# The order of TensorE's work in the attention of a gated hybrid block: equal blocks of queries, other work in fixed shares

## The chip, the cores and the metric

The kernel runs on one core of one Trainium2 chip. The metric is the device time of one execution in microseconds; lower is better. Engines are named as the profile names them: PE is TensorE (PEld its weight loads), DVE is VectorE, ACT is ScalarE, POOL is GpSimd, and SP issues the DMAs.

## The reference

One layer over 1024 positions of width 1024, float32. After an RMS norm one wide projection gives all inputs of two branches: an mLSTM in both directions (4 heads of 256), and a differential attention (8 heads). Both branches are gated, projected, mixed by two sigmoid gates, and projected once more onto the residual. The change lies in the attention:

```python
def diff_attention(q, k, v, lam):
    ...
    def one_block(qb):
        scores = jnp.einsum('bqhjd,bkhjd->bhjqk', qb, k) * scale
        p = jax.nn.softmax(scores, axis=-1)
        p_diff = p[:, :, 0] - lam * p[:, :, 1]
        return jnp.einsum('bhqk,bkhd->bqhd', p_diff, v)
...
dq = apply_rope(b_q.reshape(B, S, DA_HEADS, 2, DA_QK_DIM), positions)
dk = apply_rope(b_k.reshape(B, S, DA_HEADS, 2, DA_QK_DIM), positions)
...
att = diff_attention(dq, dk, da_v, lam)
att = rmsnorm(att, da_subln_g[layer]) * (1.0 - lambda_init)
y_b = att.reshape(B, S, DA_WIDTH).astype(x.dtype) * jax.nn.silu(b_z)
```

Each head has two score maps (j = 0, 1) of 64 dimensions each, two softmaxes, one difference of them, and one product with v.

## The kernel before, in words

Every float32 product is made as three products of a high and a low part (`H`, `L`). The kernel runs in stages: the norm and the first projections; the mLSTM's inputs; the attention of 8 heads; the mLSTM; the rest of the gates; the two branch products, the mix and the output product.

**Units.** `build` (L1429) puts PE's work together as a list of `Unit`s (L46): a cost in us of PE, a function that issues the instructions, and names by which a planner knows them. `MM` = 0.214 is the cost of one matmul of 512 columns, `TP` = 0.109 that of a transpose. `run` (L386) goes through the finished list in order; it loads a weight block one key ahead of its first use (`load_w`, L177: a DMA, a cast on ACT, a subtraction on POOL). In the attention only PE's order is written by hand; the order on ACT, DVE and POOL is chosen by the framework when the program is built.

**The attention's units of head h** (`da_parts`, L906), for a block t of 128 queries:

- S(t), L923: twelve matmuls for both score maps into two PSUM tiles of two banks each (tag `S`); then on DVE two maxima over 1024 keys (L926), on ACT two exponentials (L928), on DVE the difference (L932 to L934). Cost 6 MM.
- T(t, g), g = 0 and 1, called T0 and T1: four transposes (L131) of the difference into one bank of tag `T`; ACT copies the high part (`pH`, L947), DVE takes the low part (`pL`, L948).
- PV(pair, g), called PV0 and PV1: twelve matmuls each (L959) of two blocks of queries with v; both write one bank of tag `T`, which ACT copies to `att` (L961) at the end.
- M(pair): two transposes of `att` into a bank of tag `T`, and two squares on ACT in place (L971), with sums; behind the fourth M of a head POOL makes the norm and multiplies the gate `zg` by `att` (L975 to L981).
- G(half): four transposes that spread the norm into a bank of tag `T`; DVE multiplies it into `zg` (L991), and SP stores `zg`.

There are two banks of tag `T` for T, PV, M and G together, and two of tag `pj` for all projections.

**The block's order** (`da_cycle`, L1006): S(t) of this head first; M at even t; G of the head before at t = 4 and 5; PV0 and PV1 at odd t; then T0 and T1 of the block before. M(2), M(3) and the last PV of a head fall into the next head's blocks 0 to 2.

**The other work** of a head is a list of its own, in this order: the rope projections of q and k of the next head (`da_proj`, L842: 32 units of 3 MM, in two halves of 512 positions; behind each half come products on DVE, L852 to L864, sums and differences on POOL, L865 to L869, casts on ACT, L868, and DMAs); for odd heads the projection of v for two heads (`da_v`, 32 units of 6 TP); for even heads the z projections (L880, L881) of the head before, ahead of the rope, and of this head, behind it; z of head 0 is made before the attention; head 0 takes one gate projection, head 7 three (`gate_units`, L831).

**The planner** (`Weaver`, L62) holds a model of the time. `weave` merges the main list of a head (the units of the eight blocks, one behind the other) with the other list: at each step it puts the unit that is ready first, and among those ready the one that is less far on in its own list by cost. `ready` (L68) knows of named predecessors with a lag each (`after`, `LAG`) and of banks: a unit with a tag isn't ready before one of the tag's banks is free, by the model's `hold` of its last users (2.2 us for T and G, 3.7 for PV, 8.1 for M). `put` adds a unit to the list and moves the model's time on.

Of the kernel before, what the change touches and what calls it, by code (L numbers as in the profile page):

```python
# [13 lines left out]

S = 1024
D = 1024
# [3 lines left out]
L = 256  # L20
NC = S // L
NB = L // 128
# [6 lines left out]
def two_pi_parts():  # L29
# [9 lines left out]
MM = 0.214  # L39
TP = 0.109  # L40

LAG = dict(Th=2.2, Sh=5.0, PVh=3.7, Mh=8.1, qk=14.0, T=6.8, PV=3.7, M=4.5, F=6.0, TTh=1.9, TT=3.2, POh=1.6,
           PO=1.7, Wh=0.3, W=2.0, STh=2.1, ST=4.9, th=1.8, t=4.1, aq=9.0, outh=6.6, out=14.0, G=6.0)
# [18 lines left out]
class Weaver:  # L62
# [28 lines left out]
    def weave(self, *lists):  # L91


        lanes = {}
        for i, un in enumerate(lists):
            total, c = sum(u.cost for u in un) or 1.0, 0.0
            for u in un:
                lanes.setdefault((i, u.lane), []).append((c / total, u))
                c += u.cost
        self.coming = {u.name for un in lists for u in un if u.name}  # L100
        heads = list(lanes.values())
        while heads:
            best = min(heads, key=lambda l: (max(self.ready(l[0][1]), self.now), l[0][0]))
            u = best.pop(0)[1]
            self.put(u)
            self.coming.discard(u.name)
            heads = [l for l in heads if l]


class Block:  # L110
# [199 lines left out]
    def big(self, n, dt=F32):  # L310
        return self.s0.tile([128, S + 4], dt, name=n, tag="big", bufs=6)

# [30 lines left out]
    def conv_sink(self, seg, n):  # L343
# [3 lines left out]
        def sink(i, j, ps, rest):  # L347
            if i not in box:
                box[i] = (self.big("cin"), [])
                p.memset(box[i][0][:, 0:2], 0.0)  # L350
                p.memset(box[i][0][:, S + 2:S + 4], 0.0)
            raw, got = box[i]
# [9 lines left out]
            w = lambda j: self.conv[:, j * 16 + base:j * 16 + base + 1]  # L362
            y = self.big("y")[:, 0:S]
            for half in range(2):
# [247 lines left out]
    def angles(self, an):  # L612
# [38 lines left out]
        for src in (cs, sn):  # L651
            reps.append(self.big("rep")[:, 0:S].rearrange("p (k a b) -> p k a b", k=8, a=4))
            for k in (0, 4):
# [252 lines left out]
    def da_parts(self, h, st):  # L906
        v, a, p, q, w1 = self.v, self.a, self.p, self.q, self.w1

        def scores(t):
            if t == 0:  # L910
                st["Z"] = w1.tile([128, 2, 8], F32, name="Z", tag="Z", bufs=2)
                st["ms"] = w1.tile([128, 8], F32, name="ms", tag="ms", bufs=2)
                st["att"] = w1.tile([128, S], F32, name="att", tag="att", bufs=1)
            qq, k = st["q", t // 4], st["k"]
            c = slice((t % 4) * 128, (t % 4) * 128 + 128)
            Z = st["Z"]
            both = [self.bank("S", (128, S)) for _ in range(2)]

            for o in (slice(0, 512), slice(512, S)):
                for m, (x, y) in enumerate(((0, 0), (0, 1), (1, 0))):  # L920
                    for j, ps in enumerate(both):
                        r = slice(64 * j, 64 * j + 64)
                        self.t.matmul(ps[:, o], lhsT=qq[r, x, c], rhs=k[r, y, o], start=(m == 0), stop=(m == 2))  # L923
            for j, ps in enumerate(both):
                nm = w1.tile([128, 1], F32, name="nm", tag="nm", bufs=3)
                v.tensor_reduce(out=nm, in_=ps, axis=AX.X, op=ALU.max, negate=True)  # L926
                e = w1.tile([128, S], F32, name=f"e{j}", tag=f"e{j}", bufs=2 if j == 0 else 1)
                a.activation(out=e, in_=ps, func=AF.Exp, bias=nm[:, 0:1], accum_out=Z[:, j, t:t + 1])  # L928
                st["e", j] = e
            e0 = st["e", 0]  # L930
            r = w1.tile([128, 1], F32, name="r", tag="r", bufs=1)
            v.reciprocal(out=r, in_=Z[:, 1, t:t + 1])  # L932
            v.tensor_scalar(out=r, in0=r, scalar1=Z[:, 0, t:t + 1], scalar2=self.nlam[:, 0:1], op0=ALU.mult, op1=ALU.mult)
            v.scalar_tensor_tensor(out=e0, in0=e, scalar=r[:, 0:1], in1=e0, op0=ALU.mult, op1=ALU.add)  # L934
            st["p", t] = e0

        def transposes(t, g):
            pt = st["p", t]
            s = slice((t % 2) * 128, (t % 2) * 128 + 128)
            if t % 2 == 0:  # L940
                st["pT", t // 2, g] = (w1.tile([128, 4, 256], F32R, name="pH", tag="pH", bufs=2),
                                       w1.tile([128, 4, 256], F32R, name="pL", tag="pL", bufs=2))
            pH, pL = st["pT", t // 2, g]
            ps = self.bank("T", (128, 4, 128))
            for i in range(4):
                self.tr(ps[:, i, :], pt[:, (4 * g + i) * 128:(4 * g + i + 1) * 128])
            a.copy(pH[:, :, s], ps)  # L947
            v.tensor_tensor(out=pL[:, :, s], in0=ps, in1=pH[:, :, s].bitcast(F32), op=ALU.subtract)  # L948
# [14 lines left out]
        def squares(t2):  # L963
            pt = self.bank("T")
            for i in range(2):
                t = 2 * t2 + i
                self.tr(pt[:, i * 128:(i + 1) * 128], st["att"][:, t * 128:(t + 1) * 128])
            for i in range(2):
                t = 2 * t2 + i
                x = pt[:, i * 128:(i + 1) * 128]  # L970
                a.activation(out=x, in_=x, func=AF.Square, accum_out=st["ms"][:, t:t + 1])  # L971
            if t2 == 3:
                zz = w1.tile([128, 8], F32, name="zz", tag="zz", bufs=1)
                Z0 = st["Z"][:, 0, :]
                p.tensor_scalar(out=zz, in0=Z0, scalar1=EPS, scalar2=None, op0=ALU.mult)  # L975
                p.tensor_tensor(out=zz, in0=zz, in1=Z0, op=ALU.mult)
                rs = self.rsqrt(w1, st["ms"], 1.0 / 128.0, zz, "rb", eng=p)
                p.tensor_scalar(out=rs, in0=rs, scalar1=(1.0 - LAMBDA_INIT) * 0.5, scalar2=None, op0=ALU.mult)
                for half in range(2):
                    g = st["g", half]  # L980
                    p.tensor_tensor(out=g, in0=st["att"][:, half * 512:(half + 1) * 512], in1=g, op=ALU.mult)  # L981
                st["rs"] = rs

        def scale(half):
# [3 lines left out]
            for i in range(4):  # L988
# [3 lines left out]
            q.dma_start(out=self.yb[h][:, half * 512:(half + 1) * 512], in_=g)  # L992

        return dict(
            S=lambda t: Unit(6 * MM, lambda: scores(t), tag="S", hold=LAG["Sh"], name=("S", h, t), after=((("qk", h), LAG["qk"]),)),
            T=lambda t, g: Unit(4 * TP, lambda: transposes(t, g), tag="T", hold=LAG["Th"], name=("T", h, t, g),
                                after=((("S", h, t), LAG["T"]),)),
            PV=lambda t2, g: Unit(12 * TP, lambda: pv(t2, g), tag="T" if g == 0 else None, hold=LAG["PVh"], name=("PV", h, t2, g),
                                  after=((("T", h, 2 * t2 + 1, g), LAG["PV"]),)),
            M=lambda t2: Unit(2 * TP, lambda: squares(t2), tag="T", hold=LAG["Mh"], name=("M", h, t2),  # L1000
                              after=((("PV", h, t2, 1), LAG["M"]), (("z", h if t2 == 3 else -1), 0.0))),
            G=lambda half: Unit(4 * TP, lambda: scale(half), tag="T", hold=LAG["Th"], name=("G", h, half),
                                after=((("M", h, 3), LAG["F"]),)))
# [425 lines left out]
    def build(self):  # L1429
# [21 lines left out]
        with pool(name="const", bufs=1) as self.const, \  # L1451
# [51 lines left out]
            w = Weaver()  # L1503
            w.add(enter("h", "hpool"), enter("tab", "tab", side="right"), enter("tf", "tf", side="right"),
                  enter("p0", "p0", side="right"), banks("ps0", T=6), keep(E.PE, E.Activation, E.DVE, E.Pool), do(begin))
            k = self.PIECES
# [30 lines left out]
            for i, x in enumerate(products + [None]):  # L1537
                y = products[i - 1] if i else None
                un = sum(([x[0]] if x else []) + ([y[6]] if y else []) + ([x[3]] if x else []) + ([y[5]] if y else [])
                         + ([x[1], x[4], x[2]] if x else []), [])  # L1540
# [5 lines left out]
            qk, z = zip(*[self.da_proj(h, sts[h]) for h in range(NH_B)])  # L1546
            w.add(do(lambda: setattr(self, "ahead", True)), *qk[0], *z[0], *self.da_v(0, sts[0:2]))
            prev = None
            for h in range(NH_B):
                cur = self.da_parts(h, sts[h])  # L1550
                main = sum((self.da_cycle(cur, prev, t) for t in range(8)), [])
                ahead = qk[h + 1] if h + 1 < NH_B else []
                if h + 1 == NH_B:
                    nxt = fill(FILL[h]) + z[h]
                elif h % 2 == 1:
                    nxt = ahead + self.da_v((h + 1) // 2, sts[h + 1:h + 3]) + fill(FILL[h])
                else:
                    nxt = z[h - 1] + ahead + fill(FILL[h]) + z[h] if h else ahead + fill(FILL[0])
                w.weave(main, nxt)
                prev = cur  # L1560
            end = sum((self.da_cycle(None, prev, t) for t in range(6)), [])
            w.weave(end[:-2], fill(2))
# [25 lines left out]
            k = len(passA) // 2  # L1588
# [52 lines left out]
```

## Time and profile before

| | us |
|---|---|
| median of 3 runs | 1708.58 |
| the runs | 1706.8 to 1708.61 |
| the profiled execution, its own time | 1706.56 |
| its span, from the first to the last instruction | 1704.7 |
| the attention's eight heads in it | about 455 to 1075 |

The mean clock granted to PE is 0.994. In a row of the timeline the first number is the start in us from the span's beginning, the second the duration; then the engine, the line of the kernel, the operation, the tile written and the tiles read, the count, and in brackets the idle time of the engine just before and what ended it. Matmuls overlap in their pipeline, so the distance from start to start tells their price, not the duration. In the tile names S are scores, T is any bank of tag `T` (T<-ident,att is M, T<-ident,rb_y is G, T<-ident,e is T0 or T1), and pj is a projection.

### The profile page before, as it was taken

How to read it: one execution, taken by the hardware profiler on the slowest of the kernel's cores; microseconds unless marked ns; L12 is line 12 of the kernel's file. 1: busy time of each engine (PE TensorE's matmuls, PEld its weight loads, DVE VectorE, ACT ScalarE, POOL GpSimd, SP SyncE). 2: the span in 40 equal slices, each digit the busy share in tenths (PEclk: the TensorE clock that was granted, in tenths of full speed). 3: DMA queues.
4: the chain of work that ended last, by engine and by line, in shares of the span. 5: the costliest groups of instructions: out<-in, count | busy, mean ns of one | idle time of the engine just before them, and what ended most of it. 6: DMA issues, size and time to landing. Idle time of an engine off the chain costs nothing. (4 is left out here: it accounts for less than half of the span.)

```text
span 1704.7 us, 25425 instructions
## 1 busy us (share of the span) xinstructions
PE 1654.3 (97%) x9431; PEld 1389.8 (82%) x9431; DVE 988.3 (58%) x1799; ACT 777.0 (46%) x1554; POOL 606.5 (36%) x680
## 2 busy tenths in 40 slices
PE   7999999999999999999999999999999899999998
PEld 5777887887877987898788878899999777888887
DVE  5778668674377666666666655226666633135533
ACT  7454555553265455454545455325655644022221
POOL 5767676665243134413241331221330312212000
PEclk9999999999999999999999999999999999999999
DMA  5334444334231213221231222175464327344222
GB/s 181 98 121 130 137 123 132 116 124 146 65 81 44 63 38 87 56 69 38 75 81 32 62 62 75 50 208 155 143 170 137 109 89 237 117 147 136 87 91 83
DMA packets 175630, 178.79 MB, mean 105 GB/s; under 512 B 12185, under 2 KB 135410, under 8 KB 175506
## 3 DMA queue, kind: packets, MB, share of 16 engines
q1 hardware_dynamic: 174594, 175.58, 34.5%
q8 instruction: 74, 1.21, 0.3%
q10 hardware_dynamic: 912, 1.59, 0.2%
q14 instruction: 50, 0.41, 0.1%
HBM read 114.11 MB, written 46.24 MB: 94 GB/s over the span
## 5 line engine op out<-in xcount | busy, mean ns | idle before, releaser
L429 PE MATMUL pj<-hH,wH 128*128 128x512 f32 x640 | 266.8, 417 | 3.3 <-ACT f L542 1.5
L429 PE MATMUL pj<-hH,wL 128*128 128x512 f32 x640 | 252.0, 394 | 1.8 <-POOL wL L207 1.8
L429 PE MATMUL pj<-hL,wH 128*128 128x512 f32 x640 | 250.8, 392 | 0.2 <-DVE hL L580 0.2
L209 POOL TENSOR_TENSOR wL<-raw,wH 128x1024 fp32r<-128x1024 f32 x41 | 99.7, 2431 | 291.9 <-ACT wH L204 289.5
L928 ACT ACTIVATE e<-S,nm 128x1024 f32<-128x1024 f32 x128 | 142.5, 1115 | 96.1 <-DVE nm L926 96.0
L926 DVE TENSOR_REDUCE nm<-S 128x1 f32<-128x1024 f32 x128 | 150.5, 1218 | 8.5 <-PE S L923 7.8
L429 PEld LDWEIGHTS pj<-hH,wH 128*128 128x128 f32 x640 | 121.0, 189 | 37.9 <-issue 14.5
L451 PE MATMUL pj<-wH,hH 128*128 128x256 f32 x512 | 149.9, 293 | 0.3
L948 DVE TENSOR_TENSOR pL<-T,pH 128x512 fp32r<-128x512 f32 x128 | 87.9, 689 | 105.8 <-ACT pH L947 104.9
L451 PE MATMUL pj<-wL,hH 128*128 128x256 f32 x512 | 144.8, 283 | 1.4 <-POOL wL L207 1.4
L429 PEld LDWEIGHTS pj<-hH,wL 128*128 128x128 f32 x640 | 120.6, 188 | 30.3 <-POOL wL L207 3.2
L451 PE MATMUL pj<-wH,hL 128*128 128x256 f32 x512 | 144.5, 282 | 0.0
L429 PEld LDWEIGHTS pj<-hL,wH 128*128 128x128 f32 x640 | 121.3, 190 | 18.3 <-DVE hL L580 0.6
L429 PE MATMUL pj<-sl_yb,wH 128*128 128x512 f32 x384 | 121.8, 397 | 4.4 <-ACT sl_yb L1314 2.2
L947 ACT CAST pH<-T 128x512 fp32r<-128x512 f32 x128 | 74.8, 585 | 84.6 <-PE T L131 84.0
L204 ACT CAST wH<-raw 128x1024 fp32r<-128x1024 f32 x56 | 58.9, 1052 | 114.3 <-PE pj L429 88.1
L923 PE MATMUL S<-kst,qq 64*128 64x512 f32 x768 | 106.7, 408 | 0.0
L451 PEld LDWEIGHTS pj<-wH,hH 128*128 128x128 f32 x512 | 97.7, 191 | 5.5 <-issue 2.2
L451 PEld LDWEIGHTS pj<-wL,hH 128*128 128x128 f32 x512 | 97.5, 190 | 2.3 <-POOL wL L207 2.3
L451 PEld LDWEIGHTS pj<-wH,hL 128*128 128x128 f32 x512 | 97.7, 191 | 0.1
L429 PEld LDWEIGHTS pj<-sl_yb,wH 128*128 128x128 f32 x384 | 73.3, 191 | 22.5 <-DVE sl_yb L1315 3.3
L923 PEld LDWEIGHTS S<-kst,qq 64*128 64x128 f32 x768 | 67.8, 184 | 26.3 <-issue 10.5
(358 smaller groups left out, 4112.2 us busy)
## 6 DMA issues: line engine op xcount, KB each, us to landing
raw<-in_w_in_dram SPq DMA_DIRECT2D x88, 512.0 KB, 3.9
kst<-hl SPq DMA_DIRECT2D x64, 128.0 KB, 2.4
qq<-hl SPq DMA_DIRECT2D x64, 128.0 KB, 2.4
x<-in_x_dram SPq DMA_DIRECT2D x8, 512.0 KB, 6.1
cak<-y SPq DMA_DIRECT2D x16, 256.0 KB, 2.3
cakH<-cin SPq DMA_DIRECT2D x16, 256.0 KB, 4.4
cakL<-tz SPq DMA_DIRECT2D x16, 256.0 KB, 4.1
gm<-oz SPq DMA_DIRECT2D x16, 256.0 KB, 2.7
```

Of the source, the lines that this page charges most:

```text
L204: self.a.copy(wH, raw)
L209: self.p.tensor_tensor(out=wL, in0=raw, in1=wHf, op=ALU.subtract)
L429: self.t.matmul(ps, lhsT=l[:, k, :], rhs=r, start=(n == 0), stop=(n == 23))
L451: self.t.matmul(ps[:, i, :], lhsT=l, rhs=r[:, k, :], start=(kh == 0 and k == 0 and m == 0), stop=(kh == 1 and k == 3 and m == 2))
L923: self.t.matmul(ps[:, o], lhsT=qq[r, x, c], rhs=k[r, y, o], start=(m == 0), stop=(m == 2))
L926: v.tensor_reduce(out=nm, in_=ps, axis=AX.X, op=ALU.max, negate=True)
L928: a.activation(out=e, in_=ps, func=AF.Exp, bias=nm[:, 0:1], accum_out=Z[:, j, t:t + 1])
L947: a.copy(pH[:, :, s], ps)
L948: v.tensor_tensor(out=pL[:, :, s], in0=ps, in1=pH[:, :, s].bitcast(F32), op=ALU.subtract)
```

## The change

`weave` isn't used for the eight heads any more. A new method, `blocks`, takes the main units as eight blocks, and the other list. It gives each block the same length: the cost of all units of the head divided by eight. What a block's own units leave of that length is its room, and the room is dealt out behind its units in fixed shares: 2.0 behind S, 3.0 behind M, 0.5 behind G, none behind PV0, 1.5 behind PV1, 2.5 behind T0, 3.5 behind T1. Units of the other list are put, in their order, as long as half the next one's cost fits into what the shares have opened so far. `ready` isn't asked; what is left is added at the end. The cost of S in the planner goes from 6 MM to 8 MM. The units themselves, the order within a block, the other lists and all code after the attention stay.

```diff
+    SHARE = {"S": 2.0, "M": 3.0, "G": 0.5, "PV0": 0.0, "PV1": 1.5, "T0": 2.5, "T1": 3.5}
+
+    def blocks(self, blocks, other):
+
+        other = list(other)
+        length = (sum(u.cost for un in blocks for u in un) + sum(u.cost for u in other)) / len(blocks)
+        done = 0.0
+        for n, un in enumerate(blocks):
+            share = [self.SHARE.get(u.name[0] + (str(u.name[3]) if len(u.name) > 3 else ""), 0.0) if u.name else 0.0 for u in un]
+            main = sum(u.cost for u in un)
+            room, given = (n + 1) * length - done - main, 0.0
+            for k, u in enumerate(un):
+                self.put(u)
+                upto = room * sum(share[:k + 1]) / sum(share)
+                while other and given + other[0].cost / 2 <= upto:
+                    given += other[0].cost
+                    self.put(other.pop(0))
+            done += main + given
+        self.add(*other)
...
-            S=lambda t: Unit(6 * MM, lambda: scores(t), tag="S", hold=LAG["Sh"], name=("S", h, t), after=((("qk", h), LAG["qk"]),)),
+            S=lambda t: Unit(8 * MM, lambda: scores(t), tag="S", hold=LAG["Sh"], name=("S", h, t), after=((("qk", h), LAG["qk"]),)),
...
-                main = sum((self.da_cycle(cur, prev, t) for t in range(8)), [])
+                main = [self.da_cycle(cur, prev, t) for t in range(8)]
...
-                w.weave(main, nxt)
+                w.blocks(main, nxt)
```

## The prediction

> **What bounds the kernel now.** I read the page first, then the busy time of the attention's stretch, then who PE waits for, then the timelines around each wait.
>
> ```profile
> span 1704.7 us, 25425 instructions
> PE 1654.3 (97%) x9431; PEld 1389.8 (82%) x9431; DVE 988.3 (58%) x1799; ACT 777.0 (46%) x1554; POOL 606.5 (36%) x680
> ```
> ```profile
> 455.00:1075.00 620.00, 614.08 (x3898) 508.81 (x3897) 402.53 (x553) 313.70 (x650) 198.52 (x188) 1.00 0.23 62
> ```
> ```profile
> PE T L131 <- ACT T L971: 5.6, 6, 1.4
> PE T L131 <- DVE pL L948: 0.3, 1, 0.3
> ```
>
> The second fence is the stretch of all eight heads: length, then busy time of PE, weight load, DVE, ACT, POOL; the granted clock is 1.00. PE is the bound. It is idle for 620.00 - 614.08 = 5.9 us, and the two waits make up just that (5.6 + 0.3): six times a transpose (T) waits for a PSUM bank that the squares (L971, on ACT) of an M unit still hold. Nothing else in the attention is there to be won, since the change neither adds nor removes a matmul.
>
> One of the six, head 1, block t = 2:
>
> ```profile
> 538.35 1.66 PE L923 MATMUL S<-kst,qq 64*128 64x512 f32 x12
> 538.44 0.69 DVE L948 TENSOR_TENSOR pL<-T,pH 128x512 fp32r<-128x512 f32 x1 [0.45 <-ACT pH L947]
> 539.04 0.68 DVE L863 TENSOR_TENSOR hl<-pj,sinT 128x512 f32<-128x512 f32 x1
> 539.94 0.50 PE L429 MATMUL pj<-hH,wH 128*128 128x512 f32 x1
> 542.10 0.38 PE L131 MATMUL T<-ident,att 128*128 128x128 f32 x2
> 542.90 1.11 ACT L928 ACTIVATE e<-S,nm 128x1024 f32<-128x1024 f32 x1
> ```
> ```profile
> 545.26 0.39 PE L429 MATMUL pj<-hH,wL 128*128 128x512 f32 x1
> 546.29 0.65 PE L131 MATMUL T<-ident,e 128*128 128x128 f32 x4 [0.64 <-ACT T L971]
> ```
> ```profile
> 546.04 0.20 ACT L971 ACTIVATION_READ_ACCUMULATOR T<-T 128x1 f32 x1
> ```
>
> I count from the end of the scores S, here 539.94, where the first filler matmul starts. M (T<-ident,att) stands at 2.16, its squares end at 546.24 = 6.30, since ACT takes them behind both exponentials, and these (from 2.96) behind the rope copies of the next head's projection. T1 could have started at 545.26 + 0.23 = 545.49 = 5.55, so it loses 0.80, 0.16 more than the idle column shows, because the last matmul's modelled end runs on. With that, the six cost 5.6 + 6 x 0.16 = 6.6, the last 0.3 about 0.4: **7.0 us is all that can go.**
>
> **The change, part by part.** S's cost goes from 6 to 8 MM (1.712), which only feeds the planner's sums. The diff touches no line of z, so "all z in the attention" moves nothing by itself. What changes is the order: the old weave asked ready() before each unit and so kept T away from held banks; blocks() asks nothing and deals the other units by fixed shares. The other list keeps its own order, so the weights' keys, their loads, copies and subtractions stay in sequence, and SP's queue sees the same loads; yb's stores still wait for their own L991. The matmuls themselves cost what they did: 64 score groups, each between fillers of full height.
>
> The orders, by arithmetic. Head 2: main 8 x 1.712 + 16 x 0.436 + 8 x 1.308 + 4 x 0.218 + 2 x 0.436 = 32.9, other 64 x 0.642 = 41.1, so a block has 74.0 / 8 = 9.25. Block 4 has room 5.80 and shares S 2, M 3, G 0.5, T0 2.5, T1 3.5 of 11.5, which open 1.01, 2.52, 2.77, 4.03, 5.80. A unit goes out while given + 0.32 is within that: two after S, two after M (2.57 given), none after G (2.57 + 0.32 > 2.77), two, three. So: S 2 M 2 **G T0** 2 T1 3. Heads 1 to 7 all come out so at t = 4. Blocks 0 and 2: S 2 M 3 T0 2 T1 3; block 6: S 2 M 2 T0 3 T1 3; odd blocks: S 1 (G) PV0 PV1 1 T0 2 T1 2.
>
> *G then T0 at t = 4 (new).* There are two T banks. M holds one, G the other, and T0 comes directly. Rows of block 4 now, head 2 and then head 7 (no rope there):
>
> ```profile
> 639.51 0.50 PE L429 MATMUL pj<-hH,wH 128*128 128x512 f32 x1
> 640.98 0.38 PE L131 MATMUL T<-ident,att 128*128 128x128 f32 x2
> 641.12 0.48 PE L429 MATMUL pj<-hH,wH 128*128 128x512 f32 x1
> 641.89 0.60 PE L131 MATMUL T<-ident,rb_y 128*128 128x128 f32 x4
> 642.25 0.49 PE L429 MATMUL pj<-hH,wH 128*128 128x512 f32 x1
> 642.48 1.11 ACT L928 ACTIVATE e<-S,nm 128x1024 f32<-128x1024 f32 x1
> 642.60 0.75 DVE L991 SCALAR_TENSOR_TENSOR zg<-zg,cols,T 128x512 f32<-128x512 f32 x1 [0.45 <-PE T L131]
> 643.58 0.27 ACT L971 ACTIVATE T<-T 128x128 f32<-128x128 f32 x1
> 643.87 1.10 ACT L928 ACTIVATE e<-S,nm 128x1024 f32<-128x1024 f32 x1
> ```
> ```profile
> 645.15 0.19 ACT L971 ACTIVATION_READ_ACCUMULATOR T<-T 128x1 f32 x1
> ```
> ```profile
> 1039.84 0.50 PE L429 MATMUL pj<-hH,wH 128*128 128x512 f32 x1
> 1041.19 1.11 ACT L928 ACTIVATE e<-S,nm 128x1024 f32<-128x1024 f32 x1 [1.36 <-DVE nm L926]
> 1042.22 0.60 PE L131 MATMUL T<-ident,rb_y 128*128 128x128 f32 x4
> 1042.93 0.75 DVE L991 SCALAR_TENSOR_TENSOR zg<-zg,cols,T 128x512 f32<-128x512 f32 x1 [0.64 <-PE T L131]
> ```
> ```profile
> 1043.87 0.19 ACT L971 ACTIVATION_READ_ACCUMULATOR T<-T 128x1 f32 x1
> ```
>
> Two filler units behind S take 640.98 - 639.51 = 1.47; a third 0.69 (2.16 above). M (0.14) and one unit behind it (0.77) take 0.91, to 641.89; M and two 1.60. So G starts at 3.07. Its four transposes hand over after 0.36 (642.25), M's two after 0.14 (641.12), which is 0.11 each, 0.44 for four where a transpose follows: T0 could start at 3.51. G's bank is free when L991 ends, 643.35 - 641.89 = 1.46 after G's start (head 7: 1.46): 4.53. M's is free at 645.34 - 639.51 = 5.83 with rope and 1044.06 - 1039.84 = 4.22 without. T0 loses 0.7 (M's bank, head 7) to 2.3 (M's, with rope), by G's bank 1.02. I take 1.0, since the rows now show T0 on G's bank: seven heads, **+7.0**. Behind T0 stand on PE's queue T1, the fillers and the next scores, and ACT's copy of T0 waits for it; nothing hides it. A gain is excluded, for both banks are held.
>
> *T1 behind M, t = 2 of heads 1, 3, 5.* M now stands at 1.47, where the first square goes between the exponentials (fence above), and squares end 645.34 - 642.48 = 2.86 after the first exponential starts. T1 stands at 1.47 + 0.91 + 1.38 + 0.36 + 0.77 + 0.69 = 5.58, as now. But two units instead of one stand between the last T1 and S, so L863 isn't held up behind pL (538.44) and starts some 0.5 earlier: exponential from 2.96 - 0.5, squares end near 5.3. Three waits of 0.8 go: **-2.4** (bounds -2.4 to 0).
>
> *T1 at t = 4 of heads 1, 3, 5 (new).* There ACT is latest:
>
> ```profile
> 558.59 1.66 PE L923 MATMUL S<-kst,qq 64*128 64x512 f32 x12
> 559.67 2.40 POOL L209 TENSOR_TENSOR wL<-raw,wH 128x1024 fp32r<-128x1024 f32 x1 [6.68 <-ACT wH L204]
> 560.19 0.38 PE L451 MATMUL pj<-wH,hH 128*128 128x256 f32 x1
> 565.11 1.11 ACT L928 ACTIVATE e<-S,nm 128x1024 f32<-128x1024 f32 x1
> 567.90 0.20 ACT L971 ACTIVATION_READ_ACCUMULATOR T<-T 128x1 f32 x1
> ```
>
> The rope projection ends as S starts, and its POOL work waits behind a 2.40 us subtraction; the exponential comes 6.52 later. In the new order one unit (0.7) lies between: exponential at 6.52 - 0.7 - 1.60 = 4.2, squares end 7.1, T1 at 4.53 + 1.82 = 6.35. Three times 0.7: **+2.0** (0 if POOL takes the rope first; 7.91 - 6.35 = 1.6 each, 4.7, if nothing moves). Now T1 comes late enough not to care.
>
> *T1 at t = 6 of heads 2, 4, 6.* Now 1.3 us each:
>
> ```profile
> 657.68 0.60 PE L131 MATMUL T<-ident,e 128*128 128x128 f32 x4
> 658.41 2.54 POOL L194 TENSOR_TENSOR wL<-raw,wH 128x512 fp32r<-128x512 f32 x2 [8.93 <-ACT wH L193]
> 660.50 0.50 PE L429 MATMUL pj<-hH,wH 128*128 128x512 f32 x1
> 663.99 1.11 ACT L928 ACTIVATE e<-S,nm 128x1024 f32<-128x1024 f32 x1
> 667.38 0.66 PE L131 MATMUL T<-ident,e 128*128 128x128 f32 x4 [1.13 <-ACT T L971]
> ```
>
> The rope projection ends at 657.68, the exponential comes 6.31 later. In the new order it ends right at S's start: exponential at 6.31 - 1.60 = 4.7, squares 7.6, T1 at 5.58, a loss of 2.0; or none, if POOL isn't on the subtraction first. Between 0 and 2.0 I keep 1.3, the row itself: **0** (-3.9 to +2.1).
>
> *Head 0* has M at 0.78 and T1 at 4.20 against squares at 4.22 (head 7's): its 0.4 goes: **-0.4**.
>
> **Sum:** 7.0 + 2.0 - 2.4 + 0 - 0.4 = **+6.2** on the profiled execution's 1706.56: 1712.8. The median of the runs (1708.58) stands 2.0 above that execution, so 1714.8.
>
> **Rivals.** *Faster:* ACT takes both squares between the exponentials. M at 1.47 is ready near 1.9, the first exponential ends at 1.35 + 1.2, both squares by 3.5, T0's time. Then no bank is late anywhere: -7.0, 1701.6. For it: the first square does go there; against: the second doesn't in either fence. It decides from squares ending before 3.6. *No change:* G's wait is 0.7 (M's bank), POOL takes the rope first at t = 4, part of the t = 6 wait goes: 4.9 - 2.4 - 0.4 - 1.3 = +0.8, 1709.4. *Heavier:* T0 is given M's bank, whose squares end at 7.1, 5.8 and 4.2: 3 x 3.6 + 3 x 2.3 + 0.7 = 18.4, T1 then free; with -2.4 - 0.4 and up to +2.1 that is +17.7, 1726.3. *The clock falls:* the waits make PE's clock drop for a while. If the way from T0 to T1 (1.82) ran at half speed behind each of the seven, that is 7 x 1.82 = 12.7 more, 1727.5. Against it: the stretch was granted 1.00 with six waits of 0.8 to 1.5 in it. The Trainium skill, "TensorE: Matmul & The Clock Gate", section "A second HAM failure mode: psum-queue depth-cycling", speaks for it: short idle times between matmul groups over cycled banks are said to make the clock fall and recover again and again. By that page's window of about 3.4 us at half speed it would be some 12 us, as an estimate. *The change does nothing:* equal block lengths could only help where the bank of the scores or an engine is late, and no wait row names S; so that part is worth 0 in any case.
>
> **How the numbers follow.** Forecast 0.50 (1711 to 1720), no change 0.20, faster 0.17, heavier 0.11, the clock 0.02. About 0.2% (3.4 us) is what a measurement tells apart here: faster is below 1705.2, slower above 1712.0. From the forecast's low end and the no-change case's edges: faster 0.18, same 0.21, slower 0.61. The range 1702 to 1724 leaves out the ends of the faster and the heavier case, and the clock.
>
> **What would show it.** Right: the waits of T L131 rise from 5.9 to about 12 us of idle, seven of them on L991 or L971 directly behind G's transposes at t = 4, and the 0.64 waits of t = 2 are gone. Wrong: PE idle in the attention below 6 us, squares both ahead of the second exponential, or T waits of 2 us and more at t = 4.

## The result and the profile after

The changed kernel takes 1737.09 us (median of 4 runs, 1733.03 to 1739.1) against 1707.69 (4 runs, 1706.58 to 1708.61): a ratio of 1.0169, 95% interval 1.0149 to 1.019. It is slower, as forecast, but by 29 us instead of 6. In the changed kernel the lines of the attention stand 22 further down (the transposes T at L153, the squares of M at L993, the copy of PV's bank at L983, the multiplication of G's bank into zg at L1013).

The profiled execution took 1736.52 us; its page begins like this:

```profile
span 1734.7 us, 25454 instructions
PE 1666.3 (96%) x9431; PEld 1395.7 (80%) x9431; DVE 994.7 (57%) x1799; ACT 781.0 (45%) x1554; POOL 608.9 (35%) x680
```

The span grew by 1734.7 - 1704.7 = 30.0 us. PE has the same 9431 matmuls, but 12.0 us more of busy time: not only were waits added, the matmuls themselves took longer. The waits of PE in the attention (engine, line and what it waited for; us in total, times, longest):

```profile
PE T L153 <- ACT T L993: 18.5, 10, 3.3
PE T L153 <- ACT att L983: 3.8, 2, 2.9
```

Idle time for T went from 5.9 to 22.3 us, and a second line has appeared, for PV's bank. Next the attention in windows, and three of the five stretches in it for which the granted clock was 0.50 (length, busy time of PE, PEld, DVE, ACT, POOL, granted clock, DMA share, GB/s):

```profile
455.00:1100.00 645.00, 622.66 (x3859) 511.18 (x3857) 406.09 (x548) 314.34 (x644) 200.19 (x186) 0.98 0.23 60
503.65:510.48 6.83, 6.13 (x22) 4.38 (x22) 3.79 (x5) 1.72 (x5) 1.27 (x1) 0.50 0.63 160
571.91:578.74 6.83, 5.91 (x28) 5.91 (x29) 3.11 (x5) 2.10 (x7) 0.00 (x0) 0.50 0.77 190
1015.65:1019.06 3.41, 3.41 (x10) 2.19 (x10) 2.16 (x4) 0.76 (x2) 1.17 (x1) 0.50 0.82 190
```

Before, the clock was granted in full in the whole attention; such a stretch at half clock is called a fall of the clock below. The other two stretches lie at 739.17 and 906.42 and are 6.8 us long, with 5.76 and 5.57 us of PE in them. If half of PE's time in a stretch is lost, that is (6.13 + 5.91 + 5.76 + 5.57 + 3.41) / 2 = 13.4 us. This is an estimate, and the upper end of one, as the matmuls' distances in the next fences show.

Now one place of the new order, block t = 4 of head 1, in the timeline:

```profile
564.12 1.66 PE L945 MATMUL S<-kst,qq 64*128 64x512 f32 x12
565.71 0.39 PE L473 MATMUL pj<-wH,hH 128*128 128x256 f32 x1
568.89 0.60 PE L153 MATMUL T<-ident,rb_y 128*128 128x128 f32 x4
569.53 0.75 DVE L1013 SCALAR_TENSOR_TENSOR zg<-zg,cols,T 128x512 f32<-128x512 f32 x1 [1.36 <-PE T L153]
569.92 1.11 ACT L950 ACTIVATE e<-S,nm 128x1024 f32<-128x1024 f32 x1
571.30 1.10 ACT L950 ACTIVATE e<-S,nm 128x1024 f32<-128x1024 f32 x1
572.59 0.19 ACT L993 ACTIVATION_READ_ACCUMULATOR T<-T 128x1 f32 x1
572.83 1.11 PE L153 MATMUL T<-ident,e 128*128 128x128 f32 x4 [3.34 <-ACT T L993]
573.96 0.41 PE L473 MATMUL pj<-wH,hL 128*128 128x256 f32 x1
574.17 0.41 PE L473 MATMUL pj<-wL,hH 128*128 128x256 f32 x1
```

G starts at 568.89; T0 could follow at 568.89 + 0.44 = 569.33. G's bank is free when its reader ends, at 569.53 + 0.75 = 570.28. T0 starts at 572.83, just behind the end of M's second square, at 572.59 + 0.19 = 572.78. So T0 has M's bank, and 572.83 - 569.33 = 3.50 us are lost. The filler matmuls behind it stand 574.17 - 573.96 = 0.21 us apart; those of the same kind ahead of it stood 568.78 - 568.66 = 0.12 apart:

```profile
568.66 0.28 PE L473 MATMUL pj<-wH,hL 128*128 128x256 f32 x1
568.78 0.28 PE L473 MATMUL pj<-wL,hH 128*128 128x256 f32 x1
```

That is the clock's fall at 571.91, within the wait. By these distances 0.09 of 0.21 is lost in a fall, not half; the five would then cost about 11.5 us. In the same way as the 3.50 (from the start that was possible to the start that came) the losses of the attention are:

| place | times | each, us | sum, us | forecast, us |
|---|---|---|---|---|
| T0 behind G, t = 4, heads 1, 3, 5 | 3 | 3.50 | 10.5 | 3.0 |
| the same, heads 2, 4, 6 | 3 | 1.06 | 3.2 | 3.0 |
| the same, head 7 | 1 | 0.73 | 0.7 | 1.0 |
| T1, t = 4, heads 1, 3, 5 | 3 | 0 | 0 | 2.0 |
| T1, t = 2, heads 1, 3, 5 | 3 | 0 | 0 | 0 |
| T1, t = 6, heads 2, 4, 6 | 3 | 1.85, 1.83, 2.06 | 5.7 | 4.1 |
| T1 behind PV1, head 0, t = 3 and 5 | 2 | 1.10, 3.02 | 4.1 | 0 |

Together 24.2 us (10.5 + 3.2 + 0.7 + 5.7 + 4.1), against the prediction's 7.0 of before: +17.2. With 11.5 to 13.4 from the clock that is 28.7 to 30.6, for 30.0 measured.

The last row, which the prediction didn't have, in the timeline of head 0, t = 5:

```profile
501.09 0.40 PE L451 MATMUL pj<-hH,wL 128*128 128x512 f32 x1
501.21 0.62 ACT L890 CAST hl<-m 128x512 fp32r<-128x512 f32 x1 [3.12 <-POOL m L888]
501.74 1.11 ACT L950 ACTIVATE e<-S,nm 128x1024 f32<-128x1024 f32 x1
503.93 0.37 ACT L983 COPY att<-T 128x256 f32<-128x256 f32 x1
504.35 1.12 PE L153 MATMUL T<-ident,e 128*128 128x128 f32 x4 [2.86 <-ACT att L983]
```

ACT's copy of PV's bank stands behind two exponentials, these behind rope casts, and the last of the casts waited 3.12 us for POOL. PE could have gone on at 501.09 + 0.23.

### The profile page after: what moved, and what is told of

Its sections match the earlier page's. It is cut to its first block, busy times and chain, and to the rows that moved or that the text cites. A ratio compares the mean times of both kernels' runs of the same rounds, so it can differ in the third digit from the quotient of the medians.

```text
span 1734.7 us, 25454 instructions
## 1 busy us (share of the span) xinstructions
PE 1666.3 (96%) x9431; PEld 1395.7 (80%) x9431; DVE 994.7 (57%) x1799; ACT 781.0 (45%) x1554; POOL 608.9 (35%) x680
## 5 line engine op out<-in xcount | busy, mean ns | idle before, releaser
L451 PE MATMUL pj<-hH,wH 128*128 128x512 f32 x640 | 270.6, 423 | 3.3 <-ACT f L564 1.5
L473 PE MATMUL pj<-wH,hH 128*128 128x256 f32 x512 | 153.9, 301 | 0.6 <-DVE vL L1057 0.3
L153 PE MATMUL T<-ident,e 128*128 128x128 f32 x512 | 80.5, 281 | 22.3 <-ACT T L993 18.5
L153 PEld LDWEIGHTS T<-ident,e 128*128 128x128 f32 x512 | 64.1, 144 | 38.5 <-ACT T L993 21.5
```

The lines of the kernel that those rows point to most:

```text
L153: self.t.transpose(out, in_, self.ident[0:k, 0:k])
L451: self.t.matmul(ps, lhsT=l[:, k, :], rhs=r, start=(n == 0), stop=(n == 23))
L473: self.t.matmul(ps[:, i, :], lhsT=l, rhs=r[:, k, :], start=(kh == 0 and k == 0 and m == 0), stop=(kh == 1 and k == 3 and m == 2))
```

## The experiments

Theory: PE loses what it loses because T0 (t = 4), T1 (t = 6) and T1 (head 0) are put before ACT has emptied the bank that they get, and the long ones of these waits let the clock fall. Rivals: the cost of S in the planner; T0 waits for G's bank; equal lengths as such; the clock falls for another reason.

**The cost alone.** In the kernel before, the planner's cost of S, nothing else:

```diff
-            S=lambda t: Unit(6 * MM, lambda: scores(t), ...
+            S=lambda t: Unit(8 * MM, lambda: scores(t), ...
```

> One part alone: the planner of the kernel before with the scores' cost at 8 MM. Bank theory (the loss is transposes that wait for a T bank which ACT has not yet emptied, plus the clock that falls behind the longest of these waits): weave still asks ready(), so T stays away from held banks, 1704 to 1712 us, PE idle in the attention 4 to 9 us, no fall of the clock there. Rival (the new costs, and with them the lengths, are what costs): 1720 us or more.

It took 1707.79, ratio 1.0008 (0.9999 to 1.0017). Its waits:

```profile
PE T L131 <- ACT T L971: 5.4, 6, 1.3
```

Six waits as before, at other places (three of 1.44 lost at t = 4 now). The cost of S isn't what made the kernel slower.

**One and three units between G and T0.** In the changed kernel, with N = 1 or 3 behind the first half's G, taken from what the later shares would have given:

```diff
                 self.put(u)
+                for _ in range(N if u.name[0] == "G" and u.name[2] == 0 and other else 0):
+                    given += other[0].cost
+                    self.put(other.pop(0))
```

> The changed kernel with one other unit put between G and T0 at t = 4 of heads 1 to 7. Waits fall by 0.77 us each, to 2.7 in heads 1, 3, 5 and 0.3 in heads 2, 4, 6, together 5.3 us. If a wait of 2.7 us still lets the clock fall: 1731 us. If the fall needs 3 us of idle time: 1723 us. If T0 waits for G's bank, not for M's squares, the waits stay as they are: 1737 us.

> The changed kernel with three of the other units put between G and T0 at t = 4 of heads 1 to 7, and fewer behind T0. T0 then stands about 2.2 us later on PE. If T0 waits for M's squares: its idle time falls from 3.5 to about 1.3 us in heads 1, 3 and 5 and from 1.06 to 0 in heads 2, 4, 6 and 7, together 10.6 us of waits. Bank theory with the clock: the three falls of the clock at t = 4 go too (2.8 to 2.9 us each), about 1737 - 10.6 - 8.6 = 1718 us. Waits alone, the clock being of no weight: 1726 us. If equal lengths are what costs: 1735 us or more.

One unit: 1725.84, ratio 1.0107 (1.0092 to 1.0123). Three units: 1716.85, ratio 1.0069 (1.0051 to 1.0087). The waits of the first, then T0 of head 1 at t = 4 in its timeline:

```profile
PE T L156 <- ACT T L996: 13.8, 9, 2.6
```
```profile
572.49 0.66 PE L156 MATMUL T<-ident,e 128*128 128x128 f32 x4 [2.65 <-ACT T L996]
```

and of the second:

```profile
PE T L156 <- ACT T L996: 8.9, 6, 1.9
```
```profile
572.07 1.09 PE L156 MATMUL T<-ident,e 128*128 128x128 f32 x8 [1.21 <-ACT T L996]
```

A unit is 0.7 us, and G's bank is free 0.95 us after T0 could start: by that bank one unit should leave 0.25 and three nothing. In heads 1, 3 and 5, 2.80 were left with one and 1.36 with three, so each unit took 0.7 off the 3.50: T0 waits for M's squares, in these versions too. Three units took 10.3 us of waits away and 20 us of time. The rest is the clock: it no longer falls at t = 4, nor in head 6 at t = 6, and the fall in head 0 is 3.41 us long instead of 6.83. With one unit it fell at one of the three waits of 2.80 only, and the time lies between the two forecasts.

**M ahead of S.** In the changed kernel, the order within a block, with the share of M given to S:

```diff
-        if cur:
-            un.append(cur["S"](t))
...
+        if cur:
+            un.append(cur["S"](t))
...
+            if un[0].name[0] == "M":
+                share[0:2] = [0.0, share[0] + share[1]]
```

> The changed kernel with M put ahead of S in its block, M's share going to S, so that T0 and T1 stand where they stood. The squares then run on ACT before the block's exponentials. Bank theory with the clock: all waits on squares go (20.2 us) and four of the five falls of the clock (10.4 us): 1737 - 30.6 = 1706 us, with head 0's two waits on the copy of PV's bank and one fall of the clock left (about 7 us). Waits alone: 1717 us. If equal lengths are what costs: 1725 us or more.

1706.64, ratio 1.0005 (0.9996 to 1.0014): the forecast of 1706 came true, and the loss of the change is gone. The window of heads 1 to 7, then what waits PE has left, all in head 0 and at the turn to head 1:

```profile
526.00:1072.00 546.00, 545.83 (x3489) 454.24 (x3487) 356.35 (x487) 281.69 (x576) 172.88 (x168) 1.00 0.23 61
```
```profile
PE T L155 <- ACT att L985: 3.6, 2, 2.7
PE T L155 <- DVE pL L972: 1.4, 3, 0.8
```

PE is busy for 545.83 of 546.00 us. The lengths are equal and the shares fixed as in the changed kernel; what differs is the order of M and S, so that M's squares reach ACT ahead of the exponentials of the same block. So equal lengths as such cost nothing in these heads, and the squares account for all their waits. Head 0 keeps its 2.88 us of loss at t = 5, and behind it the clock falls (507.09 to 513.92).

**M ahead of S, in the old weave.** The same swap of lines in the kernel before.

> The kernel before with M put ahead of S in its block, nothing else. Bank theory: its six waits on squares (6.6 us) go: 1700 to 1703 us. If the banks are not what makes PE wait, or if the planner only moves the waits elsewhere: 1706 to 1710 us.

1705.39, ratio 0.9998 (0.9989 to 1.0007): missed. The waits for the squares are gone, but the profile has a new one, on the scores:

```profile
PE S L923 <- ACT e L928: 2.1, 3, 0.7
```
```profile
548.07 1.19 PE L923 MATMUL S<-kst,qq 64*128 64x512 f32 x8 [0.69 <-ACT e L928]
```

S of t = 3 in heads 1, 3 and 5 comes too early, behind a short block 2, and the scores' banks are still held by the exponentials. The losses fell from 7.0 to 3.5 only. This is where equal blocks help: in heads 1 to 7 of the version before this one, which has them, no such wait occurs.

**Head 0 by the old weave.** M ahead of S everywhere, equal blocks for heads 1 to 7 only:

```diff
-                w.blocks(main, nxt)
+                w.blocks(main, nxt) if h else w.weave(sum(main, []), nxt)
```

> M ahead of S in equal blocks as in the run m_first, but head 0, whose rooms are small, is merged by weave as before. Bank theory: in m_first heads 1 to 7 had no wait at all and head 0 had five (6.1 us) and one fall of the clock (about 3 us); these go: 1706 - 9 = 1697 to 1699 us. If head 0's waits only move, or if equal blocks cost something of their own: 1703 us or more.

1705.29, ratio 0.999 (0.998 to 0.9999): missed by 6 us. Head 0's waits went, one new one came:

```profile
PE T L155 <- DVE pL L972: 1.5, 1, 1.5
```

At the turn to head 1, M now directly follows T1 of head 0 and waits until DVE has read a transpose's bank (1.67 lost); 0.7 was lost 2.2 us before it, and the clock falls (520.94 to 524.36). With up to 1.7 us for the fall these make up some 4 of the 6 us missed; the rest stays open.

**PV ahead of S too.** M and both PV ahead of S, in odd blocks for PV:

```diff
+        pvs = cur if t >= 3 else prev
+        if cur and pvs and t % 2 == 1:
+            un += [pvs["PV"](((t - 1) // 2 - 1) % 4, g) for g in range(2)]
+        if cur:
+            un.append(cur["S"](t))
...
-        if own and t % 2 == 1:
+        if own and t % 2 == 1 and not cur:
...
+            if un[0].name[0] == "PV":
+                share[0:3] = [0.0, 0.0, sum(share[0:3])]
```

> As m_first, and PV0 and PV1 ahead of S in the odd blocks, their share going to S, so that ACT copies PV's bank before the block's exponentials. Bank theory: head 0's two waits for that copy (4.0 us) and the fall of the clock (about 3 us) go, the waits of M for the low part of T1 (2.1 us) may stay: 1698 to 1702 us. If PV then waits for the low parts of the transposes instead: 1706 us or more.

1726.01, ratio 1.0111 (1.0097 to 1.0125): missed, the second case of the forecast came. The waits, then one of PV's in head 0:

```profile
PE T L985 <- DVE pL L974: 12.5, 9, 2.4
PE T L157 <- DVE pL L974: 4.2, 9, 0.6
```
```profile
497.72 0.68 DVE L974 TENSOR_TENSOR pL<-T,pH 128x512 fp32r<-128x512 f32 x1
498.45 0.39 PE L985 MATMUL T<-pH,vH 128*128 128x256 f32 x1 [2.40 <-DVE pL L974]
```

PV has come too close to the transposes. Its first matmul reads their high part only, and yet starts when DVE has taken the low part (497.72 + 0.68 = 498.40): that instruction is the last to read a transpose's bank, and PV writes one of the two banks. The low part is the input of PV's next matmul besides, so the two causes can't be told apart here. M can go ahead of S because in heads 1 to 7 the banks and its input were ready there; PV can't.

**The rope's sums on DVE.** In the changed kernel, the two lines of the rope that POOL does, given to DVE, to bring the exponentials forward:

```diff
-            p.tensor_tensor(out=m[0], in0=m[0], in1=fb(hl[:, 2]), op=ALU.subtract)
-            p.tensor_tensor(out=m[1], in0=fb(hl[:, 3]), in1=m[1], op=ALU.add)
+            v.tensor_tensor(out=m[0], in0=m[0], in1=fb(hl[:, 2]), op=ALU.subtract)
+            v.tensor_tensor(out=m[1], in0=fb(hl[:, 3]), in1=m[1], op=ALU.add)
```

> The changed kernel with the rope's two sums (L865 and L866 before) on DVE instead of POOL, nothing else. If the exponentials are late because ACT stands in the rope's casts, and these behind POOL's weight subtraction: T0 at t = 4 of heads 1, 3, 5 waits 1.1 instead of 3.5 us, T1 at t = 6 of heads 2, 4, 6 at most 0.3 instead of 1.9 us, four falls of the clock go: 1737 - 13 - 10 = 1714 us. If POOL is not the cause: 1733 us or more.

1721.72, ratio 1.0095 (1.0079 to 1.0111); forecast 1714. The waits:

```profile
PE T L153 <- ACT T L993: 13.4, 10, 2.6
```

The direction holds: 15 us come back, T1's loss at t = 6 goes from 2.06 to 1.39 in head 6 and below 1.0 in heads 2 and 4, that of head 0 at t = 5 from 3.02 to 1.29, and of the falls only one is left (894.78 to 898.2). But at t = 4 the loss only goes from 3.5 to 2.8. In the timeline of head 1, DVE's first sum takes 2.14 us, the second 0.68:

```profile
560.98 2.40 POOL L231 TENSOR_TENSOR wL<-raw,wH 128x1024 fp32r<-128x1024 f32 x1 [6.76 <-ACT wH L226]
561.79 2.14 DVE L887 TENSOR_TENSOR m<-m,hl 128x512 f32<-128x512 f32 x1
563.85 0.68 DVE L888 TENSOR_TENSOR m<-hl,m 128x512 f32<-128x512 f32 x1
```

It ends 0.55 us after POOL's subtraction (561.79 + 2.14 = 563.93 against 560.98 + 2.40 = 563.38), as if it had waited for most of it. The other sums in this trace bear that out. Beside eight of the 32 a subtraction on POOL ran for most of the time; these took 1.10 to 2.63 us, and each ended 0.55 us after the subtraction. The other 24 took 0.67 to 0.69. The Trainium skill, "SBUF — State Buffer", section "SBUF: two separate sides", says that a DVE instruction with two inputs from SBUF waits for the whole of a GpSimd instruction that reads SBUF, since both use one pair of ports. These rows agree. So the subtraction stays in the way when the sums leave POOL.

**What the runs point to.** Equal blocks for heads 1 to 7, M ahead of S in blocks 2, 4 and 6 only, head 0 as before:

```diff
+            if n and un[1].name[0] == "M":
+                un = [un[1], un[0]] + un[2:]
+                share[0:2] = [0.0, share[0] + share[1]]
...
-                w.blocks(main, nxt)
+                w.blocks(main, nxt) if h else w.weave(sum(main, []), nxt)
```

> Equal blocks for heads 1 to 7 with M ahead of S at t = 2, 4 and 6 only; at t = 0 M stays behind S, as in the change; head 0 is merged by weave, in the order of the kernel before. Bank theory: of mix0's waits those of 1.7 and 0.7 us and its fall of the clock (1.7 us) go, head 0's 0.6 of before stays: about 4 us below mix0, 1701 to 1703 us, 0.2 to 0.3% faster than the kernel before. If the waits only move: 1705 us or more.

1702.22 against 1706.38, ratio 0.9977 (0.9968 to 0.9986): as forecast, and 0.2% faster than the kernel before. The window of the attention, and block 4 of head 1 in the timeline:

```profile
455.00:1068.00 613.00, 612.43 (x3890) 507.30 (x3889) 404.95 (x550) 317.56 (x649) 195.84 (x188) 1.00 0.24 63
```
```profile
558.68 0.38 PE L156 MATMUL T<-ident,att 128*128 128x128 f32 x2
559.00 1.66 PE L948 MATMUL S<-kst,qq 64*128 64x512 f32 x12
559.68 0.20 ACT L996 ACTIVATION_READ_ACCUMULATOR T<-T 128x1 f32 x1
563.55 0.60 PE L156 MATMUL T<-ident,rb_y 128*128 128x128 f32 x4
563.99 0.60 PE L156 MATMUL T<-ident,e 128*128 128x128 f32 x4
564.58 1.11 ACT L953 ACTIVATE e<-S,nm 128x1024 f32<-128x1024 f32 x1
```

M's squares end 1.2 us after M starts, long before the exponentials, and T0 follows G at 563.99 - 563.55 = 0.44 without a wait. PE idles for 0.6 us in all eight heads, at full clock.

## Why the prediction was right and wrong

**Right.** T0 directly behind G waits in all seven heads, and this is the largest term. The waits at t = 2 went, as forecast: M stands a unit earlier, and ACT takes a square between the exponentials. In the timeline of head 1, t = 2:

```profile
545.53 0.50 PE L451 MATMUL pj<-hH,wH 128*128 128x512 f32 x1
547.91 1.11 ACT L950 ACTIVATE e<-S,nm 128x1024 f32<-128x1024 f32 x1
550.58 0.19 ACT L993 ACTIVATION_READ_ACCUMULATOR T<-T 128x1 f32 x1
551.16 0.60 PE L153 MATMUL T<-ident,e 128*128 128x128 f32 x4
```

Counted from 545.53 the first exponential comes at 2.38 (2.46 forecast), the squares end at 5.24 (near 5.3), and T1 stands at 5.63 without a wait (5.58). The cost of S did nothing by itself. The forecast that slower was likeliest held, too. Against the +6.2 of its sum, T0 behind G cost 7.4 us more, head 0 4.1 more, t = 6 1.6 more and T1 at t = 4 2.0 less; the clock, which was not in the sum, cost 11.5 to 13.4 and is the largest miss.

**The step that failed first: which bank T0 gets.** The prediction took G's bank, at 1.0 each, "since the rows now show T0 on G's bank". They do show that for the kernel before: in head 1 T0 starts at 565.96 there, 2.1 us before M's squares end.

```profile
565.96 0.60 PE L131 MATMUL T<-ident,e 128*128 128x128 f32 x4
567.90 0.20 ACT L971 ACTIVATION_READ_ACCUMULATOR T<-T 128x1 f32 x1
```

There fillers lay between G and T0. A bank is given when the program is built, and the programs built from the two kernels show which: M, G, T0 and T1 of head 1 at t = 4 have the banks 7, 6, 6, 7 before and 7, 6, 7, 6 after. In all seven heads T0 has G's bank before and M's after, and M's also where three units lie between. So the rival called heavier came true in its mechanism (3.50 where it had 3.6 for heads 1, 3 and 5; 1.06 where it had 2.3 for heads 2, 4 and 6, since their squares end 4.6 us after the scores' end and not 5.8). The prediction had the price and gave it 0.11. Why the framework picks that bank stays open. T1 then has G's bank, and the +2.0 put on it was 0.

**The second: the clock.** It was given 0.02 because six waits of 0.8 to 1.5 us had left the clock at 1.00. Those rows say nothing of waits of 3.5 us, and the heavier case, which has such waits, was priced without it. The two rivals aren't alternatives: the first brings the second. Taken together, at the prediction's own prices, they would have been 1726.3 + 12.7 = 1739.0. That this is near the 1737.09 is partly luck: the 12.7 stood for a fall at each of seven T0, and falls came at three of them and at two other places; T0's waits were 14.4 us and not 18.4, and head 0's 4.1 were in neither. That the waits cause the falls is borne out by the two versions with units behind G, where the falls at t = 4 went as the waits got shorter, and by where the falls stand (last section). The section of the Trainium skill that the prediction cited, "A second HAM failure mode: psum-queue depth-cycling" in "TensorE: Matmul & The Clock Gate", speaks of frequent short idle times between groups; here six short ones, spread over 620 us, left the clock alone, and single long ones made it fall. What frequent short ones do, no run here shows.

**The third: head 0.** The prediction looked at M there and not at PV. PV's bank is emptied by ACT behind the exponentials like M's, and the fixed shares put T1 where ready() would have held it back: 4.1 us and one of the falls.

**At t = 6** the middle was taken, "the row itself". Head 2 there, in the timeline:

```profile
677.41 0.40 PE L451 MATMUL pj<-hH,wL 128*128 128x512 f32 x1
679.50 0.66 PE L153 MATMUL T<-ident,e 128*128 128x128 f32 x4 [1.69 <-ACT T L993]
```

Lost are 679.50 - 677.64 = 1.86. The exponential came 4.56 after the scores' end (4.7 forecast): the arithmetic that led to 2.0 was good, and should have been kept.

## What to carry to other kernels

Put a short unit whose result is emptied by a queue that runs in order (M's squares on ACT) ahead of the unit that fills this queue with long work (the scores' exponentials), and not behind it: in the changed kernel that took 30 us off, three units of other work behind G only 20. It has to go with a spacing that fits, though: in the kernel before it gave nothing by itself, since the scores then waited. When a planner gives up its check of when banks are free, work out for every tile which bank it gets in the new order, and don't take the pairing from the old trace. Price a wait of PE that is longer than any in the trace before with a possible fall of the clock on top, which here turned 17.2 us of added waits into 30.0 us of time.

## What the runs showed of the hardware

In the attention the stretches at half clock last 3.41 or 6.83 us, and in each run their starts lie whole multiples of 3.41 us apart (571.91 - 503.65 = 68.26 = 20 x 3.413). In the attention of the kernels run here each of the seven losses of 2.88 to 3.50 us (from start to start) went with a fall, of thirteen between 2.05 and 2.8 us six did, and none of 1.86 us or less that stood alone.

What decides is how much of a loss lies in one window. Windows of 3.41 us can be laid over a trace, counted from the start of a fall in the same run, and PE's losses added up in each. All 14 falls in the attention start at the end of a window with 2.05 us or more lost (60% of it). Two windows with 2.06 and 2.07 lost had no fall behind them, and none with less had one. With the rope's sums on DVE, three waits of 2.8 us show it: the one that lay whole in a window brought a fall (894.78), and the two that were split between two windows, at most 2.07 in one of them, brought none. In the version with head 0 by the old weave, 1.67 and 0.71 us fell into the same window and together brought a fall. So for a wait between 2 and 3 us its place against these windows decides. These are the figures of one trace of each kernel.

One fall of 6.83 us costs about 3 us, one of 3.41 us up to 1.7, by the estimate of half of PE's time. The Trainium skill, "TensorE: Matmul & The Clock Gate", section "HAM oscillation — how this bites in real kernels", warns of idle times over some 3.4 us; here shorter ones were enough.

An instruction of DVE with two inputs from SBUF took 2.14 us instead of 0.68 beside a subtraction on POOL. Moving such work from POOL to DVE didn't get it out of the way of POOL's long instructions.
